# Expert panels in a fused transformer kernel: two sums per panel outside the gate stretch, a shorter routing, new clock estimates

## The chip, the cores and the metric

The kernel runs on one core of a Trainium2 chip. The metric is device time in microseconds (us) from launch to end; three runs of the kernel before took 2847.09, 2847.22 and 2847.55 us, and their median, 2847.22 us, is the time before. The profile is of one further execution.

## The reference, cut to what matters

The program is two blocks of two layers over 256 tokens of width 1024, all in float32. The change touches the last part of each layer of the second block, a product-key expert layer with 16384 experts:

```
def peer(xn, wq, k1, k2, u_tab, v_tab):
    q = (xt @ wq).reshape(t, 8, 256)                    # 8 heads, two halves of 128
    s1, s2 = scores of each half against 128 keys       # einsum with k1, k2
    v1, i1 = lax.top_k(s1, 16); v2, i2 = lax.top_k(s2, 16)
    cand = (v1[..., :, None] + v2[..., None, :]).reshape(t, 8, 256)
    sv, ci = lax.top_k(cand, 16)
    e1 = take_along_axis(i1, ci // 16); e2 = take_along_axis(i2, ci % 16)
    gates = softmax(sv)                                 # expert e1*128+e2, 8*16 per token
    hid = gelu(xi . u_tab[experts]); out = (gates * hid) @ v_tab[experts]
```

The kernel computes this densely: all 16384 hidden values of each token (the u stage), multiplied by a matrix of gates that is zero outside the chosen experts, and then times v_tab (the v stage).

## The kernel before, in words

**Panels.** All weights come in panels of 128x1024 floats, 512 KB, loaded by the SP queue (L63). To hold float32 precision at TensorE's fast rate each panel is split: ScalarE rounds it to fp32r (`whi`), VectorE subtracts (`wlo`). The activations are split the same way, `xh` and `xl`, and lie beside each other in one tile `xhl`. A product is the sum hi*xh + lo*xh + hi*xl. There are three buffers each of `whi` and `wlo`, so VectorE's `wlo` of a panel is put into its queue two panels ahead.

**Two ways to multiply a panel.** `feat` does 24 matmuls of 256 columns into half a PSUM bank, eight for each of the three products; two panels share one bank. `feat_sum` does 8 matmuls of 512 columns (`whi` against xh and xl side by side) and 8 of 256 (`wlo` against xh) into one whole bank, and the two halves are then added by a ScalarE copy and a VectorE add. The feed-forward layers use `feat_sum`; the u stage before uses `feat`.

**The u stage of a layer.** 128 panels, two experts' rows `e`, `e+1` at a time. Beside it, on a queue of chores, run: the search of the 16 best keys per head and half (`firsts`, `top16`: max, max_index, match_replace on VectorE), the routing of the two token halves (`route(0)`, `route(1)`), and then `builds`: 64 steps of 4 tokens. A step has TensorE make a 128x128 gate matrix per token (`gates`: one-hot `ohb` times one-hot `oha` into a bank), VectorE and ScalarE make the one-hots of the next step (`onehots`), and `place` put the gates of the step before into `G` (112 of the expert rows) and `H` (16). Rows whose hidden values exist already (`state["u"]`) are multiplied by the gates on VectorE, the others are copied on ScalarE; `late` does the other side when a pair of panels ends after gates exist: ScalarE's Gelu, and a VectorE multiply for the tokens (`state["t"]`) that have gates. The gates rotate over four PSUM banks, acc00, acc01, acc10, acc11; `feat` uses two banks named `w`.

**What sets the order.** Each engine runs its instructions in the order in which they were written. A `Chains` queue holds the chores as generators; at fixed points (`chains.run()`, three per panel) it issues every step whose due time has passed on a model clock (`Clock`, with `cost` as its price list): the model's end of the step before, plus 0.2 us, less the lead that the step yielded. Every compute instruction is recorded by one helper, so all show as L226.

Of the kernel before, what the change touches and what calls it, by code (L numbers as in the profile page):

```python
# [9 lines left out]
F32 = mybir.dt.float32  # L10
# [22 lines left out]
N_LANES = 4  # L33
EARLY = (0, 1)
LEAD_BUILD = 0.8
LEAD_TOP = 1.0
N_ABS = 2
MIX_ORDER = "FCRAB"
RANK_CONV = 1
RANK_PART = 1  # L40
RANK_RNN = 0
# [85 lines left out]
class Clock:  # L127
# [33 lines left out]
    def cost(self, e, op, out, ins, kw):  # L161
        n = max(math.prod(x.shape[1:]) for x in [out, *ins])
        if e == "p":
            rate = (2 if op == "transpose" else 4) if ins[-1].dtype == F32 else max(1, 256 / out.shape[-1])
            if op == "matmul" and out.shape[0] == 64:
                rate *= 0.6
            return math.prod(out.shape[1:]) * rate / 2.4e3 + 0.003
        if e == "v":
            small = sum(x.shape[1:] == (1,) for x in ins if x.shape != out.shape)
            if op == "tensor_scalar" and ins[0].space == SB:  # L170
                return 0.07 + n / 1.92e3 + 0.06 * small
            return 0.07 + n / 0.96e3 + 0.06 * small
# [116 lines left out]
def net(tc, A, out, stop=None):  # L289
# [3 lines left out]
    with ctx:  # L293
# [8 lines left out]
        def bank():  # L302
            return psum.tile([128, 512], F32, name="w", bufs=2)
# [76 lines left out]

        banks = [0]

        def feat_sum(dst, other):


            banks[0] += 1
            ps = bank() if banks[0] & 2 else other()
            hi, lo = W.get()
            for k in range(8):
                mm(ps, hi[:, k * 128:(k + 1) * 128], xhl[:, :, k], start=k == 0, stop=False)  # L390
                if k == 3:
                    chains.run()
            W.ahead("hi")
            chains.run()
            for k in range(8):
                mm(ps[:, :T], lo[:, k * 128:(k + 1) * 128], xh[:, k], start=False, stop=k == 7)
            W.ahead("lo")
            chains.run()
            nc.scalar.activation(dst, ps[:, T:], AF.Copy)
            nc.vector.tensor_tensor(dst, dst, ps[:, :T], op=OP.add)  # L400

        def nat(ps, xh, xl):

# [879 lines left out]
        def peer(l, acc, soon):  # L1283
            with tc.tile_pool(name=f"peer{l}", bufs=1) as p:
# [77 lines left out]
                def route(c):  # L1362
                    r = R[c]
                    v, i, fi, cf, ef, sv, ci, cs, cand = (r[n] for n in ("v", "i", "fi", "cf", "ef", "sv", "ci", "cs", "cand"))
                    nc.vector.tensor_copy(fi, i)
                    for b in (slice(0, 4), slice(4, 8)):
                        nc.vector.tensor_tensor(cand[:, b], v[:, 0, b][:, :, :, None].to_broadcast([128, 4, 16, 16]),
                                                v[:, 1, b][:, :, None, :].to_broadcast([128, 4, 16, 16]), op=OP.add)
                        yield
                    for h in range(8):  # L1370
                        yield from top16(sv[:, h], ci[:, h], cand[:, h].rearrange("p a b -> p (a b)"))
                        yield LEAD_TOP
                    nc.vector.tensor_scalar(cs, ci, 4, None, op0=OP.logical_shift_right)
                    nc.vector.tensor_copy(cf[:, 0], cs)
                    nc.vector.tensor_scalar(cs, ci, 15, None, op0=OP.bitwise_and)
                    nc.vector.tensor_copy(cf[:, 1], cs)
                    yield
                    for s in range(2):
                        for b in (slice(0, 4), slice(4, 8)):
                            nc.vector.tensor_tensor(cand[:, b], cf[:, s, b][:, :, :, None].to_broadcast([128, 4, 16, 16]),  # L1380
                                                    iota[:, None, None, 0:16].to_broadcast([128, 4, 16, 16]),
                                                    op=OP.is_equal)
                            yield
                            nc.vector.tensor_tensor(cand[:, b], cand[:, b],
                                                    fi[:, s, b][:, :, None, :].to_broadcast([128, 4, 16, 16]), op=OP.mult)
                            yield
                            nc.vector.tensor_reduce(ef[:, s, b], cand[:, b], axis=AX.X, op=OP.add)
                            yield
# [20 lines left out]
                state = {"u": 0, "t": 0}  # L1409

                def onehots(t0):
                    a = p.tile([128, 4, 128], F32, name="oha", bufs=2)
# [11 lines left out]

                def gates(t0, a, b):

                    i = t0 // 4 % 4
                    ps = psum.tile([128, 512], F32, name=f"acc{i // 2}{i % 2}", bufs=1)
                    for j in range(4):
                        mm(ps[:, j * 128:(j + 1) * 128], a[:, j], b[:, j], start=True, stop=True)  # L1430
                    return ps
# [23 lines left out]
                        yield LEAD_BUILD  # L1455
                    place(*last)

                def late(e, ps):

                    nt, g = state["t"], rows(e, 2)  # L1460
                    pv = ps.rearrange("p (a t) -> p a t", a=2)
                    if nt < T:
                        nc.scalar.activation(g[:, :, nt:], pv[:, :, nt:], AF.Gelu_apprx_tanh)
                    if nt:
                        nc.scalar.activation(pv[:, :, :nt], pv[:, :, :nt], AF.Gelu_apprx_tanh)
                        nc.vector.tensor_tensor(g[:, :, :nt], g[:, :, :nt], pv[:, :, :nt], op=OP.mult)
                    state["u"] = e + 2

                for work in (route(0), route(1), builds()):
                    chains.add(work, 1, 1)  # L1470
                for e in range(0, 128, 2):
                    ps = bank()
                    for j in range(2):
                        if e == 80 and j == 0:
                            while state["t"] == 0:
                                chains.idle()
                        feat(ps[:, j * T:(j + 1) * T], xh, xl)
                    late(e, ps)
                chains.drain()
                acc = acc_banks()  # L1480

                def cut(e):
# [44 lines left out]
        def aux(i):  # L1527
            return psum.tile([128, 512], F32, name=f"acc0{i}", bufs=1)
# [170 lines left out]
```

## Time and profile before

| | |
|---|---|
| median of three runs | 2847.22 us |
| the profiled execution | 2847.0 us, of which 2845.2 us span |
| TensorE matmul, busy | 2794.8 us (98%) |
| TensorE weight load, busy | 2553.3 us (90%) |
| VectorE (DVE), busy | 2045.7 us (72%) |
| ScalarE (ACT), busy | 1494.0 us (53%) |
| GpSimd (POOL), busy | 100.7 us (4%) |
| mean granted TensorE clock | 0.992 |

The u stages run from 1104.3 to 1531.1 us (first layer) and from about 2063 to 2489 us. Busy shares are averages over the whole program; a stretch has to be read on its own. Matmuls overlap, so a row's busy time is longer than the distance to the next row's start: the starts tell the pace. The same holds for VectorE.

### The profile page before, as it was taken

How to read it: one execution, taken by the hardware profiler on the slowest of the kernel's cores; microseconds unless marked ns; L12 is line 12 of the kernel's file. 1: busy time of each engine (PE TensorE's matmuls, PEld its weight loads, DVE VectorE, ACT ScalarE, POOL GpSimd, SP SyncE). 2: the span in 40 equal slices, each digit the busy share in tenths (PEclk: the TensorE clock that was granted, in tenths of full speed). 3: DMA queues.
4: the chain of work that ended last, by engine and by line, in shares of the span. 5: the costliest groups of instructions: out<-in, count | busy, mean ns of one | idle time of the engine just before them, and what ended most of it. 6: DMA issues, size and time to landing. Idle time of an engine off the chain costs nothing.

```text
span 2845.2 us, 47840 instructions
## 1 busy us (share of the span) xinstructions
PE 2794.8 (98%) x18786; PEld 2553.3 (90%) x18786; DVE 2045.7 (72%) x3710; ACT 1494.0 (53%) x2423; POOL 100.7 (4%) x104
## 2 busy tenths in 40 slices
PE   9999999999999999999999999999999999999999
PEld 9988889998887889999998888887999999988887
DVE  5556665666766889988995555569898899755555
ACT  4444545544454654447764444456444677544444
POOL 1001010000101100000000000010000000000000
PEclk9999999999999999999999999999999999999999
DMA  6445556544554344554345555543455433455554
GB/s 242 163 164 179 187 176 199 172 148 138 187 192 156 127 144 161 193 181 138 127 138 181 194 195 194 202 159 122 162 180 190 165 127 134 159 190 193 193 194 161
DMA packets 135969, 484.18 MB, mean 170 GB/s; under 512 B 17152, under 2 KB 18176, under 8 KB 135744
## 3 DMA queue, kind: packets, MB, share of 16 engines
q1 hardware_dynamic: 132064, 468.07, 48.2%
q0 software_dynamic: 3680, 13.05, 1.4%
q8 instruction: 148, 2.42, 0.3%
q14 instruction: 77, 0.63, 0.1%
HBM read 479.92 MB, written 1.15 MB: 169 GB/s over the span
## 4 chain that ended last, share of the span: by engine, by line
PE 51%; issue 13%; DVE 2%; ACT 1%; POOL 0%; DVEq 0%; POOLq 0%; ACTq 0%
PE w L226 30%; PE acc L226 19%; DVE G L226 2%; PE b L226 1%; ACT G L226 0%; ACT whi L226 0%; DVE wlo L226 0%; DVE xN L226 0%; ACT ohb L226 0%; POOL r L226 0%; POOL wlo L226 0%; ACT xhl L226 0%; POOL G L226 0%; ACT w L226 0%; DVE nm L226 0%
## 5 line engine op out<-in xcount | busy, mean ns | idle before, releaser
L226 DVE TENSOR_TENSOR wlo<-raw,whi 128x1024 fp32r<-128x1024 f32 (+1 forms) x874 | 1062.6, 1219 | 551.8 <-ACT whi L226 546.1
L226 ACT ACTIVATE whi<-raw 128x1024 fp32r<-128x1024 f32 (+1 forms) x881 | 924.4, 1053 | 673.5 <-PE acc L226 386.4
L226 PE MATMUL w<-xhl,whi 128*128 128x256 f32 (+1 forms) x6176 | 869.5, 292 | 4.4 <-ACT whi L226 4.2
L226 PEld LDWEIGHTS w<-xhl,whi 128*128 128x128 f32 x6176 | 795.4, 193 | 20.8 <-ACT whi L226 5.0
L226 PE MATMUL acc<-whi,xhl 128*128 128x512 f32 x2048 | 550.2, 390 | 2.4 <-ACT xhl L226 2.4
L226 PE MATMUL w<-xhl,wlo 128*128 128x256 f32 x3248 | 462.4, 286 | 9.4 <-DVE wlo L226 9.3
L226 PEld LDWEIGHTS acc<-whi,xhl 128*128 128x128 f32 x2048 | 384.5, 188 | 82.3 <-ACT xhl L226 2.8
L226 PEld LDWEIGHTS w<-xhl,wlo 128*128 128x128 f32 x3248 | 422.5, 193 | 15.4 <-DVE wlo L226 11.2
L226 PE MATMUL acc<-wlo,xhl 128*128 128x512 f32 x1024 | 317.7, 389 | 0.0
L226 PEld LDWEIGHTS acc<-wlo,xhl 128*128 128x128 f32 x1024 | 192.3, 188 | 39.8
L226 ACT ACTIVATE G<-w 128x512 f32<-128x512 f32 (+16 forms) x157 | 81.6, 520 | 203.1 <-PE w L226 202.6
L226 DVE TENSOR_SCALAR oha<-iota,e1T,gT 128x128 f32<-128x128 f32 x512 | 152.8, 341 | 0.0
L226 PE MATMUL acc<-ohb,oha 128*128 128x128 f32 x1024 | 136.7, 276 | 0.3
L226 PEld LDWEIGHTS acc<-ohb,oha 128*128 128x128 f32 x1024 | 125.9, 192 | 2.0 <-ACT ohb L226 1.4
L226 PE MATMUL w<-whi,xhl 128*128 128x256 f32 x640 | 121.2, 287 | 0.0
L226 PEld LDWEIGHTS w<-whi,xhl 128*128 128x128 f32 x640 | 101.9, 193 | 2.3 <-issue 2.1
L226 PE MATMUL w<-wlo,xhl 128*128 128x256 f32 x320 | 91.3, 285 | 0.3
L226 POOL TENSOR_TENSOR r<-v,minus_half 128x1 f32<-128x1 f32 x26 | 21.8, 840 | 1959.5 <-DVE v L226 1959.5
L226 ACT ACTIVATE ohb<-iota,me2T 128x128 f32<-128x128 f32 x256 | 87.5, 392 | 0.7 <-PE acc L226 0.7
L226 PE MATMUL b<-xhl,whi 128*128 128x512 f32 x320 | 80.2, 393 | 0.0
L226 DVE TENSOR_TENSOR xhl<-G,xhl 128x512 fp32r<-128x512 f32 x112 | 76.5, 684 | 0.0
L226 DVE TENSOR_TENSOR G<-G,acc 128x272 f32<-128x272 f32 (+22 forms) x128 | 66.5, 520 | 8.5 <-ACT H L226 8.2
(303 smaller groups left out, 2962.1 us busy)
## 6 DMA issues: line engine op xcount, KB each, us to landing
raw<-u SPq DMA_DIRECT2D x256, 512.0 KB, 3.2
raw<-v SPq DMA_DIRECT2D x256, 512.0 KB, 3.3
raw<-ffn SPq DMA_DIRECT2D x132, 512.0 KB, 4.0
raw<-mix SPq DMA_DIRECT2D x90, 512.0 KB, 3.3
raw<-att SPq DMA_DIRECT2D x80, 512.0 KB, 3.3
raw<-ret SPq DMA_DIRECT2D x63, 512.0 KB, 3.3
bias<-scr POOLq DMA_DIRECT2D x12, 512.0 KB, 7.1
G<-norm_g SPq DMA_DIRECT2D x4, 512.0 KB, 5.6
```

The costliest lines, as they stand in the source:

```text
L226: return f(*args, **kw)
```

## The change

1. `feat_sum` is divided; its matmuls become `feat_both`.
2. In the u stage a panel goes through `feat_both` into one of four banks (the two `w`, acc10, acc11) while no gates are being built, that is before the first `place` and after the last; ScalarE copies and VectorE adds the halves into `u`, a slice of the tile `xN` (`value`), and Gelu reads `u`. Between the first and the last `place` it is `feat`, two panels per bank, as before.
3. The gates keep the two banks acc00 and acc01 (`aux`).
4. `xN`, which holds the residual, is saved to DRAM ahead of this and loaded back after the u stage, on GpSimd's queue.
5. `route` no longer adds all 256 pairs of each head but 52 that can be among the best 16, in lists of 64; the index passes are smaller or rewritten.
6. `Clock.cost` prices max, max_index and match_replace at 0.2 us more than the size term in place of 0.07; `LEAD_TOP` goes from 1.0 to 2.0, and `route`'s steps yield a lead of 2.0.

```diff
+        if e == "v" and op in ("max", "max_index", "match_replace"):
+            return 0.2 + n / 0.96e3
...
-        def feat_sum(dst, other):
+        def feat_both(ps):
             hi, lo = W.get()
             for k in range(8):
                 mm(ps, hi[:, k * 128:(k + 1) * 128], xhl[:, :, k], start=k == 0, stop=False)
...
+        def feat_sum(dst, other):
+            banks[0] += 1
+            ps = bank() if banks[0] & 2 else other()
+            feat_both(ps)
             nc.scalar.activation(dst, ps[:, T:], AF.Copy)
             nc.vector.tensor_tensor(dst, dst, ps[:, :T], op=OP.add)
+            chains.run()
...
+                kept = dram.tile([128, 2, D], F32, name=f"kept{l}")
+                nc.gpsimd.dma_start(kept, xN)
...
+                    for o, a0, na, nb in RANKS:
+                        sh = [128, 8, na, nb]
+                        nc.vector.tensor_tensor(few[:, :, o:o + na * nb].rearrange("p h (a b) -> p h a b", a=na),
+                                                v[:, 0, :, a0:a0 + na, None].to_broadcast(sh),
+                                                v[:, 1, :, None, 0:nb].to_broadcast(sh), op=OP.add)
+                    yield LEAD_ROUTE
...
-                    i = t0 // 4 % 4
-                    ps = psum.tile([128, 512], F32, name=f"acc{i // 2}{i % 2}", bufs=1)
+                    ps = aux(t0 // 4 % 2)
...
+                def value(e, j, u, ps):
+                    nc.scalar.activation(u[:, j], ps[:, T:], AF.Copy)
+                    yield
+                    nc.vector.tensor_tensor(u[:, j], u[:, j], ps[:, :T], op=OP.add)
+                    state["b"] += 1
+                    if j:
+                        yield
+                        late(e, u)
...
                 for e in range(0, 128, 2):
-                    ps = bank()
+                    if 0 < state["t"] < T:
+                        while state["b"] < state["s"]:
+                            chains.idle()
+                        ps = bank()
+                        for j in range(2):
+                            feat(ps[:, j * T:(j + 1) * T], xh, xl)
+                        late(e, ps.rearrange("p (a t) -> p a t", a=2))
+                        continue
+                    u = hid[:, state["s"] // 2 % 4]
                     for j in range(2):
...
+                        ps = bank() if n & 2 else psum.tile([128, 512], F32, name=f"acc1{n % 2}", bufs=1)
+                        feat_both(ps)
+                        chains.add(value(e, j, u, ps), "value", 0)
                 chains.drain()
+                nc.gpsimd.dma_start(xN, kept)
```

What this does to the order is the same in both layers; all before the first u stage is unchanged on every engine. In TensorE's queue before, the stretch with gates settles to four gate groups (`ohb,oha`, four tokens each) in three panels (a panel is `whi` x8, `wlo` x8, `whi` x8; x16 spans the end of one and the start of the next):

```order
L226 MATMUL w<-xhl,whi 128x256 x16
L226 MATMUL w<-xhl,wlo 128x256 x8
L226 MATMUL acc_13341<-ohb,oha 128x128 x4
L226 MATMUL w<-xhl,whi 128x256 x16
L226 MATMUL acc_13378<-ohb,oha 128x128 x4
L226 MATMUL w<-xhl,wlo 128x256 x8
L226 MATMUL acc_13409<-ohb,oha 128x128 x4
L226 MATMUL w<-xhl,whi 128x256 x16
L226 MATMUL w<-xhl,wlo 128x256 x8
```

After, the same place has the last panels in two sums (512 columns), and then two gate groups in every panel:

```order
L230 MATMUL acc_13063<-ohb,oha 128x128 x4
L230 MATMUL acc_13058<-xhl,whi 128x512 x4
L230 MATMUL acc_13058<-xhl,wlo 128x256 x8
L230 MATMUL acc_13105<-ohb,oha 128x128 x4
L230 MATMUL w<-xhl,whi 128x256 x8
L230 MATMUL w<-xhl,wlo 128x256 x8
L230 MATMUL acc_13149<-ohb,oha 128x128 x4
L230 MATMUL w<-xhl,whi 128x256 x16
L230 MATMUL acc_13189<-ohb,oha 128x128 x4
L230 MATMUL w<-xhl,wlo 128x256 x8
L230 MATMUL acc_13220<-ohb,oha 128x128 x4
```

The groups have moved together: the 64 of a layer lie in 47 panels before and in 32 after, of which the last 30 have two each. Before, 67 panels come ahead of the first group and 14 after the last; now 77 and 19, with 96 of the 128 panels in two sums and 32 by `feat`.

In VectorE's queue before, in the same stretch, a `wlo` stands after every one or two build steps (a step is four `oha`, two `ohb` and the multiply of `place`):

```order
L226 TENSOR_TENSOR wlo<-raw,whi 128x1024
L226 TENSOR_SCALAR oha<-iota,e1T,gT 128x128 x3
L226 TENSOR_SCALAR ohb<-miota,me2T 128x128
L226 TENSOR_SCALAR oha<-iota,e1T,gT 128x128
L226 TENSOR_SCALAR ohb<-miota,me2T 128x128
L226 TENSOR_TENSOR G<-G,acc_13257 128x68x4
L226 TENSOR_TENSOR G<-G,w 128x2x16
L226 TENSOR_TENSOR wlo<-raw,whi 128x1024
```

After, two full steps stand between one `wlo` and the next throughout, and the multiply of `late` (`G<-G,w`) in every second panel:

```order
L230 TENSOR_TENSOR wlo<-raw,whi 128x1024
L230 TENSOR_SCALAR oha<-iota,e1T,gT 128x128 x3
L230 TENSOR_SCALAR ohb<-miota,me2T 128x128
L230 TENSOR_SCALAR oha<-iota,e1T,gT 128x128
L230 TENSOR_SCALAR ohb<-miota,me2T 128x128
L230 TENSOR_TENSOR G<-G,acc_14169 128x92x4
L230 TENSOR_TENSOR G<-G,w 128x2x132
L230 TENSOR_SCALAR oha<-iota,e1T,gT 128x128 x3
L230 TENSOR_SCALAR ohb<-miota,me2T 128x128
L230 TENSOR_SCALAR oha<-iota,e1T,gT 128x128
L230 TENSOR_SCALAR ohb<-miota,me2T 128x128
L230 TENSOR_TENSOR G<-G,acc_14200 128x94x4
```

## Rows read from the trace of the kernel before

**Rows 1.** Windows: length, busy us of PE, PEld, DVE, ACT, POOL; clock, DMA
```profile
1104.30:1298.00 193.70, 193.70 (x1617) 193.70 (x1617) 171.04 (x355) 95.26 (x111) 0.00 (x0) 1.00 0.53 183
1299.00:1491.00 192.00, 191.85 (x1630) 191.14 (x1630) 181.38 (x515) 142.56 (x404) 0.00 (x0) 1.00 0.38 131
```
**Rows 2.** TensorE's timeline, u stage without gates: start, busy us, engine, operation
```profile
1245.78 2.08 PE L226 MATMUL w<-xhl,whi 128*128 128x256 f32 x16
1248.66 2.08 PE L226 MATMUL w<-xhl,whi 128*128 128x256 f32 x16
```
**Rows 3.** TensorE's timeline, gate stretch: a panel with two groups, then with one
```profile
1304.08 2.16 PE L226 MATMUL w<-xhl,whi 128*128 128x256 f32 x16
...
1308.73 2.16 PE L226 MATMUL w<-xhl,whi 128*128 128x256 f32 x16
...
1312.50 2.16 PE L226 MATMUL w<-xhl,whi 128*128 128x256 f32 x16
```
**Rows 4.** The u stage's first and the v stage's first matmul, with ScalarE between
```profile
1104.26 2.16 PE L226 MATMUL w<-xhl,whi 128*128 128x256 f32 x16
...
1529.97 0.58 ACT L226 ACTIVATE w<-w 128x512 f32<-128x512 f32 x1 [1.82 <-PE w L226]
1530.47 1.14 ACT L226 ACTIVATE xhl<-G 128x512 fp32r<-128x512 f32 x2
1531.14 0.73 PE L226 MATMUL acc<-whi,xhl 128*128 128x512 f32 x2 [1.21 <-ACT xhl L226]
```
**Rows 5.** TensorE's timeline, feed-forward layer: two panels of `feat_sum`
```profile
305.93 2.00 PE L226 MATMUL b<-xhl,whi 128*128 128x512 f32 x8
...
311.52 1.78 PE L226 MATMUL w<-xhl,whi 128*128 128x512 f32 x7
```
**Rows 6.** VectorE's timeline, gate stretch: `wlo`, a step, the next step, a wait
```profile
1303.18 1.22 DVE L226 TENSOR_TENSOR wlo<-raw,whi 128x1024 fp32r<-128x1024 f32 x1
1304.32 0.85 DVE L226 TENSOR_SCALAR oha<-iota,e1T,gT 128x128 f32<-128x128 f32 x3
...
1305.73 0.43 DVE L226 TENSOR_TENSOR G<-G,acc 128x272 f32<-128x272 f32 x1
1306.08 0.85 DVE L226 TENSOR_SCALAR oha<-iota,e1T,gT 128x128 f32<-128x128 f32 x3
...
1307.77 0.44 DVE L226 TENSOR_TENSOR G<-G,acc 128x272 f32<-128x272 f32 x1 [0.18 <-ACT H L226]
```
**Rows 7.** VectorE's groups, 1104 to 1535 us: busy us, mean ns, idle before, releaser
```profile
L226 DVE TENSOR_TENSOR H<-H,w 128x512 f32<-128x512 f32 x7 | 4.8, 689 | 7.5 <-ACT w L226 7.5
L226 DVE TENSOR_TENSOR G<-G,acc 128x368 f32<-128x368 f32 x3 | 1.6, 537 | 0.4 <-ACT H L226 0.4
L226 DVE TENSOR_TENSOR G<-G,w 128x264 f32<-128x264 f32 x1 | 0.4, 417 | 0.0
```
**Rows 8.** TensorE's timeline at the first two gate groups
```profile
1297.94 1.12 PE L226 MATMUL w<-xhl,whi 128*128 128x256 f32 x8
1299.07 1.56 PE L226 MATMUL acc<-ohb,oha 128*128 128x128 f32 x8
1300.38 1.20 PE L226 MATMUL w<-xhl,whi 128*128 128x256 f32 x8
```
**Rows 9.** Feed-forward layer: ScalarE's copy and VectorE's add after a `feat_sum` panel
```profile
308.93 0.39 ACT L226 ACTIVATE g<-b 128x256 f32<-128x256 f32 x1 [1.46 <-PE b L226]
...
309.34 0.42 DVE L226 TENSOR_TENSOR g<-g,b 128x256 f32<-128x256 f32 x1 [0.62 <-ACT g L226]
```
**Rows 10.** VectorE's timeline, key searches in lists of 128: first half, second half, next
```profile
1107.41 0.29 DVE L226 MAX8 G<-G 128x8 f32<-128x128 f32 x1
...
1108.52 0.29 DVE L226 MAX8 G<-G 128x8 f32<-128x128 f32 x1
...
1109.13 0.28 DVE L226 MAX8 G<-G 128x8 f32<-128x128 f32 x1
```
**Rows 11.** DMA issues: KB each, median us from issue to landing
```profile
xN<-x POOLq DMA_DIRECT2D x1, 1024.0 KB, 12.7
```

More of the change, by code (lines that the diff above doesn't have):

```diff
@@ L35 @@
 LEAD_BUILD = 0.8
-LEAD_TOP = 1.0
+LEAD_TOP = 2.0
+LEAD_ROUTE = 2.0
 N_ABS = 2
 MIX_ORDER = "FCRAB"
+RANKS = ((0, 0, 1, 16), (16, 1, 1, 8), (24, 2, 2, 8), (40, 4, 4, 4), (56, 8, 8, 1))
 RANK_CONV = 1
@@ L381, in net @@
         banks = [0]
-        def feat_sum(dst, other):
-            banks[0] += 1
-            ps = bank() if banks[0] & 2 else other()
+        def feat_both(ps):
             hi, lo = W.get()
@@ L1365, in route @@
                     nc.vector.tensor_copy(fi, i)
[L1366 to L1369, printed above, removed]
+                    flat = cand.rearrange("p h a b -> p (h a b)")
+                    few = flat[:, :512].rearrange("p (h n) -> p h n", h=8)
@@ L1370, in route @@
+                    for o, a0, na, nb in RANKS:
[4 more added lines that the diff above has]
+                    yield LEAD_ROUTE
                     for h in range(8):
-                        yield from top16(sv[:, h], ci[:, h], cand[:, h].rearrange("p a b -> p (a b)"))
+                        yield from top16(sv[:, h], ci[:, h], few[:, h])
@@ L1372, in route @@
                         yield LEAD_TOP
[L1373 to L1377, printed above, removed]
-                    for s in range(2):
[L1379 to L1388, printed above, removed]
+                    t0, t1, t2 = (flat[:, j * 128:(j + 1) * 128].rearrange("p (h k) -> p h k", h=8) for j in range(3))
@@ new lines, in route @@
+                    ra, rb = cf[:, 0], cf[:, 1]
+                    nc.vector.tensor_copy(t0, ci)
+                    for t, n in ((t1, 3), (t2, 2)):
+                        nc.vector.tensor_scalar(cs, ci, n, None, op0=OP.logical_shift_right)
+                        nc.vector.tensor_copy(t, cs)
+                    yield LEAD_ROUTE
+                    nc.vector.tensor_scalar(t1, t1, -1.0, 0.0, op0=OP.add, op1=OP.max)
+                    nc.vector.scalar_tensor_tensor(t1, t2, -6.0, t1, op0=OP.add, op1=OP.max)
@@ new lines, in route @@
+                    nc.vector.scalar_tensor_tensor(ra, t0, -48.0, t1, op0=OP.add, op1=OP.max)
+                    yield LEAD_ROUTE
+                    nc.vector.tensor_scalar(t1, ra, 8.0, 8.0, op0=OP.mult, op1=OP.add)
+                    nc.vector.scalar_tensor_tensor(t1, ra, 16.0, t1, op0=OP.mult, op1=OP.min)
+                    nc.vector.tensor_scalar(t2, ra, 4.0, 24.0, op0=OP.mult, op1=OP.add)
+                    nc.vector.scalar_tensor_tensor(t2, ra, 48.0, t2, op0=OP.add, op1=OP.min)
+                    nc.vector.tensor_tensor(t1, t1, t2, op=OP.min)
@@ new lines, in route @@
+                    nc.vector.tensor_tensor(rb, t0, t1, op=OP.subtract)
+                    yield LEAD_ROUTE
+                    for s in range(2):
+                        for k0, nr in ((0, 8), (8, 16)):
+                            q = flat[:, :64 * nr].rearrange("p (h k a) -> p h k a", h=8, k=8)
+                            sh, ks = [128, 8, 8, nr], slice(k0, k0 + 8)
+                            nc.vector.tensor_tensor(q, cf[:, s, :, ks, None].to_broadcast(sh),
+                                                    iota[:, None, None, 0:nr].to_broadcast(sh), op=OP.is_equal)
+                            yield LEAD_ROUTE
+                            nc.vector.tensor_tensor(q, q, fi[:, s, :, None, 0:nr].to_broadcast(sh), op=OP.mult)
+                            yield LEAD_ROUTE
+                            nc.vector.tensor_reduce(ef[:, s, :, ks], q, axis=AX.X, op=OP.add)
+                            yield LEAD_ROUTE
@@ L1407, in route @@
                     yield
-                state = {"u": 0, "t": 0}
+                state = {"u": 0, "t": 0, "b": 0, "s": 0}
                 def onehots(t0):
@@ L1456, in builds, with late @@
                     place(*last)
-                def late(e, ps):
+                def late(e, pv):
                     nt, g = state["t"], rows(e, 2)
-                    pv = ps.rearrange("p (a t) -> p a t", a=2)
                     if nt < T:
@@ L1470, in peer @@
                     chains.add(work, 1, 1)
-                for e in range(0, 128, 2):
-                    ps = bank()
-                    for j in range(2):
[L1474 to L1478, printed above, removed]
+                def value(e, j, u, ps):
[6 more added lines that the diff above has]
+                        late(e, u)
+                hid = xN.rearrange("p c (i a t) -> p (c i) a t", i=2, a=2)
+                for e in range(0, 128, 2):
+                    if e == 80:
+                        while state["t"] == 0:
+                            chains.idle()
+                    if 0 < state["t"] < T:
+                        while state["b"] < state["s"]:
+                            chains.idle()
+                        ps = bank()
[4 more added lines that the diff above has]
+                    u = hid[:, state["s"] // 2 % 4]
+                    for j in range(2):
+                        n = state["s"]
+                        state["s"] += 1
+                        while n - state["b"] > 3:
+                            chains.idle()
+                        ps = bank() if n & 2 else psum.tile([128, 512], F32, name=f"acc1{n % 2}", bufs=1)
+                        feat_both(ps)
+                        chains.add(value(e, j, u, ps), "value", 0)
                 chains.drain()
+                nc.gpsimd.dma_start(xN, kept)
                 acc = acc_banks()
```

## The prediction, made before the changed kernel had run

> **What bounds the kernel now.** Read the windows first. In the stretch of a u stage that has no gates yet, TensorE and its weight loads are busy all of 193.70 us and VectorE 171.04; in the stretch with gates TensorE 191.85 of 192.00 and VectorE 181.38, that is 94% [rows 1]. The clock is granted in full in both. Then TensorE's timeline, by starts: without gates a panel of `feat` takes 1248.66 - 1245.78 = 2.88 us [rows 2]. With gates, the panel with two groups takes 1308.73 - 1304.08 = 4.65 and the one with one 1312.50 - 1308.73 = 3.77 [rows 3], so a group costs 0.887. Of the whole stage: 128 x 2.88 + 64 x 0.887 = 425.4 us, and 1.2 of idle time ahead of the v stage make 426.6; from its first matmul to the v stage's first it takes 1531.14 - 1104.26 = 426.9 [rows 4]. So TensorE never waits for long inside the stage, though VectorE is close behind it. The reader is to see that: one engine full, a second at nine tenths, and a change that takes work from the first and gives some to the second.
>
> **The change on TensorE.** A panel in two sums takes (311.52 - 305.93) / 2 = 2.795 us where the feed-forward layer does it now [rows 5]; 16 weight loads in place of 24, but the same columns, so it gains only 0.085 us on 2.88. In the order, 96 panels of a layer go that way and 32 stay with `feat`: 96 x 2.795 + 32 x 2.88 + 56.8 (groups) = 417.3 us. TensorE alone would gain 8.1 us per layer.
>
> **The change on VectorE where gates are built.** Here the order matters more than the matmuls: the gate groups stand two to a panel for 30 panels, where four stood in three. TensorE needs 4.65 us for such a panel. VectorE, again by starts: `wlo` 1304.32 - 1303.18 = 1.14; the six one-hot instructions of a step 1305.73 - 1304.32 = 1.41; the multiply of `place` at 272 elements 1306.08 - 1305.73 = 0.35 [rows 6]. A next instruction thus starts 0.08 us ahead of the end that its row shows. The multiply grows with the rows done, in the order from 74 to 108 of them with four tokens each, mean 92: 368 elements take 537 ns [rows 7], 0.45 by starts. `late`'s multiply has from 0 to 512 elements, mean 256; 264 take 417 ns [rows 7], 0.34 by starts, in every second panel. The sum for a panel is 1.14 + 2 x 1.41 + 2 x 0.45 + 0.34 / 2 = 5.03 us, against TensorE's 4.65: 0.38 too much, 11.3 us over 30 panels. In the order before, three panels held 3 x 1.14 + 4 x (1.41 + 0.45) + 0.5 = 11.4 us on VectorE and 12.2 on TensorE, which is why nothing waits today.
>
> Can TensorE run ahead and take this excess from stock? `wlo` alone would allow it to be some 4.6 us late, since it stands two panels ahead. But a gate group needs its bank: with two banks in place of four, group k writes where group k-2 was, and the multiply that empties that bank is the last VectorE instruction of the step just ahead. So each group waits until VectorE has ended that step, and behind the group in TensorE's queue stand all later panels. I count the full 11.3. No row shows a group in want of a bank, as four were always enough; the ends are 11.3 - 4.6 = 6.7 and 11.3, and I take the upper, because the dependence is in the order itself.
>
> The Trainium skill says in "Perfetto Trace Analysis", section "Optimizing Tensor Performance", that independent matmul groups should rotate through different PSUM banks so that the evacuation of one overlaps the next. The change goes from four to two here. By that rule the 11.3 is paid in full; without it, 6.7. No run here shows either yet.
>
> **VectorE's own waits.** In the gate stretch it waits now and then for ScalarE, 0.18 us before a `place` [rows 6]; behind it, seven multiplies of `late` waited 7.5 us in all [rows 7]. ScalarE does about 1.0 (`whi`), two steps of 1.3 and half of two Gelus, 4 us in a panel of 5, but its Gelus must wait for the panel's end and `whi` stands behind them. From nothing to 0.6 us in every two panels, 0 to 9 us; I take 4, the nearest being the 0.4 us that three multiplies waited for [rows 7] and the 0.18. The first groups have their one-hots in the same step as the matmuls; before, TensorE lost 1300.38 - 1299.07 - 0.89 = 0.4 and, ahead of it, 0.2 [rows 8]. After, the `wlo` ahead of them is just issued too: up to 1.6, I take 0.5 more.
>
> **The end of the stage.** Now Gelu of the last pair follows its panel, and then the first `xhl`, 0.50 us later [rows 4]. After, a copy of 0.39 and an add of 0.42 come between panel and Gelu [rows 9], with two hand-overs of 0.04 (309.34 - 308.93 - 0.39 is 0.02): 0.9 us more, and nothing covers it.
>
> **Costed at nothing.** The stretch without gates: VectorE gets an add of 0.34 per panel and loses list work. A search takes 1108.52 - 1107.41 = 1.11 us for its first half and 1109.13 - 1108.52 = 0.61 for its second in lists of 128 [rows 10]; the 64-long lists are not in the trace and cost no more than these, and not less than the fixed part. With 77 `wlo` (87.8), 74 adds (25.2), 35 first and 36 second halves (60.8), 24 index passes (21.6: 12 like a `wlo`, 12 half) and some 53 small ones at 0.25 (13), VectorE has 208 us of work in TensorE's 77 x 2.795 = 215. So TensorE covers it, at 97%: if it did not, see the third rival. The smaller routing work does not bring the gates forward: 77 panels come ahead of them, 67 before, since the steps are priced higher and issued later, and 2.88 x 67 = 193 us became 215. The copy and Gelu on ScalarE: it was busy 95 of 194 us there [rows 1] and gets 77 x 0.3 more. The two transfers of `xN`: 1 MB, 12.7 us to land when last done [rows 11], with DMA at 0.38 to 0.53 [rows 1]; the saved copy has 50 us, the other the whole v stage; if the loads of panels are pushed back for its time, the ring of four panels (4 x 2.7 us) covers it. Uncovered, it would be up to 5 us per layer. All before the first u stage, and the v stages, keep their order.
>
> **The sum.** Per layer: 417.3 + 1.2 + 0.9 (end) + 11.3 + 0.5 + 4 = 435.2 us, against 426.9: 8.3 slower. Two layers: 16.6. The profiled execution took 2847.0 us, which is the median of the runs within 0.3, so 2847.0 + 16.6 = 2863.6. Its own bounds: without waits and with a clean start 417.3 + 2.1 + 11.3 = 430.7, 3.8 per layer, 2855; with 9 of waits, 1.6 at the start and 2 of small stalls in the first stretch 443.3, 16.4 per layer, 2880.
>
> **Rivals.**
> First, VectorE keeps up, because an instruction overlaps its neighbour more when the queue is never empty: then only TensorE's gain and the end count, 417.3 + 2.1 = 419.4, 7.5 per layer, 2832 us: faster. For it: TensorE waited for nothing in 192 us with VectorE at 94%. Against: the starts of rows 6 are those of a queue that was not empty. It decides if a panel with two groups costs VectorE under 4.65.
> Second, the banks don't bind, and the two panels of `wlo` in stock are used up first: 417.3 + 2.1 + 6.7 + 0.5 = 426.6, no change, 2846 us. Against: the bank is a wait in the order.
> Third, VectorE is short in the first stretch as well: an add waits for its ScalarE copy, 0.3 us per panel on an engine at 97%, so 0.16 over TensorE's pace; 75 panels make 12 us per layer more, 2888 us. For it: the thin cover. Against: VectorE's queue lags behind TensorE there, so the copy is done when the add's turn comes.
>
> **Chances.** The forecast 0.74, first rival 0.09, second 0.09, third 0.08. About 0.2%, 5.7 us, is what the measurement can tell from no change. Faster 0.10, same 0.10 (the second, and a little of the forecast's lower end), slower 0.80. The range from 2846 to 2880 takes in the forecast's own (2855 to 2880) and the second rival; the first and the third stay out.
>
> **What would show it.** In the new profile: panels of 2.795 us ahead of the gates, VectorE near 100% and TensorE below 95% where they are built, 5.0 to 5.3 us per panel with two groups, and waits of TensorE's groups for VectorE's `G`. Wrong if such panels take 4.65, or if TensorE waits for `wlo` ahead of the gates.

## The result: 33 us slower, twice the forecast

The changed kernel took 2880.48 us (median of four runs, 2879.64 to 2880.88), the kernel before 2847.15 in the same comparison (four runs): a ratio of 1.0112, 95% interval 1.0099 to 1.0124. Forecast were 2863.6 us and 16.6 us of loss; measured are 33.3. The direction was right, the forecast loss was half of the measured one, and the time lies 0.5 us above the 2880 us at which the stated range ended.

The profiled execution of the changed kernel has a span of 2878.4 us; the line is the page's busy time of each engine, its share and its instructions.

```profile
PE 2800.9 (97%) x17250; PEld 2475.9 (86%) x17250; DVE 2073.4 (72%) x3944; ACT 1548.6 (54%) x2611; POOL 100.0 (3%) x108
```

Over the whole span this hardly differs from before. The windows of the first u stage show where to look (columns as in [rows 1]): the stretch without gates, the stretch with two groups to a panel, and the end of the stage.

```profile
1097.74:1312.00 214.26, 214.26 (x1233) 188.59 (x1232) 191.44 (x499) 129.35 (x199) 0.00 (x0) 1.00 0.62 188
1324.20:1486.00 161.80, 149.51 (x1180) 140.51 (x1179) 152.27 (x459) 112.64 (x351) 0.00 (x0) 1.00 0.33 97
1489.00:1543.00 54.00, 53.92 (x319) 47.68 (x318) 37.70 (x48) 30.57 (x48) 0.00 (x0) 1.00 0.59 179
```

TensorE is full in the first and the third window. In the second **no engine is full**: TensorE has 92%, VectorE 94%, ScalarE 70%, at a clock granted in full. That is the sign of a loop of waits, and not of an engine that is too slow. From the last group of key scores to the v stage the first layer took 427.7 us before and 445.5 after, the second layer the same to 0.02 us: 17.8 us more in each. The part from the first gate group to the last took 191.4 us before, for 46 2/3 panels and 63 groups (TensorE alone: 46 2/3 x 2.88 + 63 x 0.887 = 190.3), and 173.8 after for 32 panels (148.0). So 25.7 us of each layer are waits there, where before there were 1.1.

The terms that came out as forecast first. The pace ahead of the gates (TensorE's timeline, as [rows 5]):

```profile
1201.99 2.00 PE L230 MATMUL acc<-xhl,whi 128*128 128x512 f32 x8
...
1204.78 1.55 PE L230 MATMUL w<-xhl,whi 128*128 128x512 f32 x6
```

2.79 us per panel, as taken from the feed-forward layer. The first matmul of the v stage (it answers the last row of [rows 4]), and the two transfers of `xN` (KB each, median us to landing):

```profile
1545.04 0.73 PE L230 MATMUL acc<-whi,xhl 128*128 128x512 f32 x2 [2.11 <-ACT xhl L230]
...
kept<-xN POOLq DMA_DIRECT2D x2, 1024.0 KB, 4.3
xN<-kept POOLq DMA_DIRECT2D x2, 1024.0 KB, 6.0
```

TensorE stood idle 2.11 us there in place of 1.21: the 0.9 that copy and add cost at the end. The transfers land in 4.3 and 6.0 us and nothing waits for them.

**The loop, in the rows.** First TensorE's timeline in the gate stretch, where [rows 3] showed 4.65 us from one panel to the next:

```profile
1339.49 1.13 PE L230 MATMUL acc<-ohb,oha 128*128 128x128 f32 x8
1340.37 2.16 PE L230 MATMUL w<-xhl,whi 128*128 128x256 f32 x16
1342.44 1.13 PE L230 MATMUL acc<-ohb,oha 128*128 128x128 f32 x8
1343.33 1.19 PE L230 MATMUL w<-xhl,wlo 128*128 128x256 f32 x8
1345.34 1.13 PE L230 MATMUL acc<-ohb,oha 128*128 128x128 f32 x8 [0.81 <-DVE G L230]
1346.22 0.48 PE L230 MATMUL w<-xhl,whi 128*128 128x256 f32 x2
...
1351.38 1.80 PE L230 MATMUL w<-xhl,whi 128*128 128x256 f32 x13
```

then ScalarE's in the same time:

```profile
1341.61 0.54 ACT L230 ACTIVATE G<-w 128x440 f32<-128x440 f32 x1 [1.49 <-PE w L230]
1342.18 0.21 ACT L230 ACTIVATE w<-w 128x72 f32<-128x72 f32 x1
1342.31 1.05 ACT L230 ACTIVATE whi<-raw 128x1024 fp32r<-128x1024 f32 x1
1343.26 0.68 ACT L230 ACTIVATE ohb<-iota,me2T 128x128 f32<-128x128 f32 x2
1343.97 0.42 ACT L230 ACTIVATE ohb<-ohb 128x256 f32<-128x256 f32 x1
1344.30 0.25 ACT L230 ACTIVATE G<-acc 128x120 f32<-128x120 f32 x1
1344.45 0.21 ACT L230 ACTIVATE H<-acc 128x64 f32<-128x64 f32 x1
```

and VectorE's `place` at its end:

```profile
1344.69 0.50 DVE L230 TENSOR_TENSOR G<-G,acc 128x328 f32<-128x328 f32 x1 [0.61 <-ACT H L230]
```

Read it as one chain. The group at 1339.49 holds TensorE for 0.88 us; behind it comes the last third of its panel, which ends at about 1341.3. ScalarE has waited 1.49 us for that end: it does the Gelu of the pair (0.70), `whi` (0.95), the one-hots (1.04) and the copies of `place` (0.39), in the order in which they are queued. Only then comes VectorE's multiply of `place`, which had waited 0.61 us; it frees the bank, and at 1345.34 TensorE starts the group that wanted this bank, after 0.81 us of waiting. From group to group 1345.34 - 1339.49 = 5.85 us, and the group that is late makes the next panel's end late. Where no pair ended, the Gelu is missing: from 1346.22 to 1351.38 it is 5.16, which is 5.85 less 0.70 within 0.01. The mean of the two is 5.50. The waits of the window (total us, times, longest) name three engines that wait for each other in a ring:

```profile
ACT G L230 <- PE w L230: 23.5, 15, 1.7
ACT whi L230 <- PE w L230: 23.3, 15, 1.7
PEld acc L230 <- issue: 19.4, 41, 1.0
PE acc L230 <- DVE G L230: 11.1, 15, 0.8
DVE G L230 <- ACT H L230: 7.8, 24, 0.7
```

Only 11.1 us of TensorE's waits carry the name of the multiply. The 19.4 us of `issue` ahead of the groups' weight loads have no releaser in the profile: the group at 1339.49 is not marked as waiting, and yet it starts 0.15 us behind the end of a multiply of `place` (1338.85 + 0.49), as the group at 1345.34 does (1344.69 + 0.50).

### The profile page after: what moved, and what is told of

It reads as the page before. It is cut to its first block, busy times and chain, and to the rows that moved or that the text cites. A ratio compares the mean times of both kernels' runs of the same rounds, so it can differ in the third digit from the quotient of the medians.

```text
span 2878.4 us, 45424 instructions
## 1 busy us (share of the span) xinstructions
PE 2800.9 (97%) x17250; PEld 2475.9 (86%) x17250; DVE 2073.4 (72%) x3944; ACT 1548.6 (54%) x2611; POOL 100.0 (3%) x108
## 5 line engine op out<-in xcount | busy, mean ns | idle before, releaser
L230 PE MATMUL w<-xhl,whi 128*128 128x256 f32 (+1 forms) x3872 | 655.3, 317 | 3.5 <-ACT whi L230 3.3
L230 PEld LDWEIGHTS w<-xhl,whi 128*128 128x128 f32 x3872 | 548.8, 192 | 44.4 <-ACT whi L230 4.1
L230 PE MATMUL w<-xhl,wlo 128*128 128x256 f32 x2480 | 355.2, 286 | 8.9 <-DVE wlo L230 8.9
L230 PEld LDWEIGHTS w<-xhl,wlo 128*128 128x128 f32 x2480 | 328.5, 192 | 22.9 <-DVE wlo L230 11.2
L230 PE MATMUL acc<-xhl,whi 128*128 128x512 f32 (+1 forms) x832 | 202.1, 384 | 0.0
L230 PE MATMUL acc<-ohb,oha 128*128 128x128 f32 x1024 | 145.0, 284 | 26.0 <-DVE G L230 22.8
L230 PEld LDWEIGHTS acc<-xhl,whi 128*128 128x128 f32 x832 | 145.9, 189 | 24.4
L230 PEld LDWEIGHTS acc<-xhl,wlo 128*128 128x128 f32 x800 | 108.7, 190 | 7.4
L230 PE MATMUL acc<-xhl,wlo 128*128 128x256 f32 x800 | 111.9, 283 | 0.0
L230 DVE TENSOR_TENSOR G<-G,acc 128x320 f32<-128x320 f32 (+17 forms) x128 | 68.6, 536 | 16.8 <-ACT H L230 15.6
```

The lines of the kernel that those rows point to most:

```text
L230: return f(*args, **kw)
```

## The experiments

The edits are shown shortened, against the changed kernel or, where it is said, against the kernel before.

Theory A was this loop, closed by the two gate banks. Theory B was that VectorE's work with its own waits sets the 5.50, whatever the banks are. The order of the instructions could be held fixed while banks changed, because these runs give the model clock a table in which a bank's name can be replaced by another; so order and banks could be varied apart.

**Four gate banks, the changed kernel's order.**

```
-  ps = aux(t0 // 4 % 2)
+  i = next of acc00, acc01, acc10, acc11   # acc1x only once no sum is pending in them
+  ps = psum.tile([128, 512], F32, name=f"acc{i // 2}{i % 2}", bufs=1)
+  clock.alias[ps.tensor.name] = f"acc0{t0 // 4 % 2}"   # the model clock still counts two
```

> The changed kernel with its gate groups on four banks again (acc00, acc01, acc10, acc11) from the third group on; every engine's order is word for word that of the changed kernel, only the bank names differ. Theory A, the loop through two banks: a panel with two groups takes 5.50 us because each second group waits for the place that empties its bank, which waits for ScalarE, which waits for the end of the panel that this very group delays. Four banks open the loop, and what is left is VectorE's own work, 5.03 to 5.2 us per panel: 9 to 14 us less per layer, 2852 to 2862 us. Theory B, VectorE's work with its waits for ScalarE sets the 5.50 whatever the banks are: 2880 +-3 us and 5.4 to 5.6 us per panel.

2855.25 us (eight runs; ratio to before 1.0028, 1.0018 to 1.0039): 25 us less than the changed kernel by a change of bank names alone. The stretch from the first gate group to the last went from 173.8 to 159.2 us. Its window, a gate group near its end, and its longest waits (from 1324 to 1470 us):

```profile
1315.21:1474.42 159.21, 159.20 (x1265) 152.32 (x1266) 159.21 (x497) 122.47 (x380) 0.00 (x0) 1.00 0.35 107
...
1463.06 1.56 PE L231 MATMUL acc<-ohb,oha 128*128 128x128 f32 x8
...
ACT G L231 <- PE w L231: 17.1, 14, 1.4
ACT whi L231 <- PE w L231: 13.5, 15, 1.3
PEld acc L231 <- DVE ohb L231: 2.2, 14, 0.2
```

The waits of TensorE for `G` are gone, VectorE is busy all of 159.21 us, and TensorE waits a little for its one-hots. TensorE's own 159.20 us of busy time hide pauses: by its pace it needs 148.0, and a gate group, whose row lasts 1.05 to 1.06 us early in the stretch, lasts up to 1.56 where its matmuls wait for VectorE's `ohb` (the last line names 2.2 us of these waits). Now, and only now, VectorE is the bound: 159.2 / 32 = 4.98 us per panel, where the forecast's sum was 5.03. Theory A holds for 14.6 of the 25.7 us; the other 11.2 stand with a VectorE that is never idle, and the run with the shorter `place` below tests them. The Trainium skill says in "Perfetto Trace Analysis", section "Optimizing Tensor Performance", that independent groups should rotate through PSUM banks; the trace agrees, at 14.6 us per layer between two banks and four.

**Two banks and four at a slower rate.** With four banks in the model clock the planner itself spreads the groups over 50 panels in place of 32. That order was run with both numbers of banks.

```
 # run 1: four banks as above, without the alias
 # run 2: ps = aux(t0 // 4 % 2); clock.alias[ps.tensor.name] = one of four names
```

> The changed kernel with two gate banks as it has, but the gate groups spread over 50 panels in place of 32, about four groups in three panels as in the kernel before. Theory A: with only every third panel holding two groups, the loop has slack, and TensorE alone counts: 78 x 2.795 + 50 x 2.88 + 56.8 + 4.2 (the first panel's score matmuls and small idle times, as before) + 0.9 at the end = 423.9 per layer against 429.6, so 5.7 less per layer, 2834 to 2840 us. Theory B gives the same here, since three panels hold 11.4 us of VectorE's work and 12.2 of TensorE's. Theory C, two banks bind at any rate: 2850 us or more, with waits of TensorE for G of over 10 us per layer.

> The same order as the run with 50 panels and two gate banks, word for word, with four gate banks. Theory A and B: within 3 us of that run, at 2834 to 2838 us, since the loop has slack there with two banks already. Theory C: 10 us or more faster than it.

Two banks took 2845.50 us (eleven runs; ratio 0.9996, 0.9986 to 1.0005), four 2832.07 (five runs; 0.9947, 0.9933 to 0.9960). The windows from first group to last, two banks and then four:

```profile
1315.83:1522.98 207.15, 204.19 (x1697) 200.77 (x1697) 192.30 (x540) 144.63 (x400) 0.54 (x1) 1.00 0.42 133
```

```profile
1316.61:1517.59 200.98, 200.84 (x1696) 199.82 (x1697) 191.32 (x540) 144.32 (x400) 0.54 (x1) 1.00 0.43 137
```

TensorE alone needs 50 x 2.88 + 63 x 0.887 = 199.9. With four banks 1.1 us are waits, as in the kernel before; with two 7.3. The first run missed its 2834 to 2840 us, so I was wrong that the loop has slack at this rate: where groups stand close, as they still do every few panels, the run with two banks falls back by 0.2 to 0.9 us each time. Four banks are 13.4 us faster than two (6.2 in the stretch of each layer), which is what theory C said of that pair; its own figure for two banks, 2850 us and more, was too high. The run with four banks is the version that beats both kernels: 14 us under the one before, 48 under the changed one.

**Part 3 alone.** The kernel before with nothing but the two gate banks.

```
-  i = t0 // 4 % 4
-  ps = psum.tile([128, 512], F32, name=f"acc{i // 2}{i % 2}", bufs=1)
+  ps = aux(t0 // 4 % 2)
```

> The kernel before with part 3 of the change alone: the gates on acc00 and acc01; every panel through feat, old routing, old prices. The model clock counts the wait for a bank into TensorE's time, so steps fall due sooner, and the gate groups come to stand over 31 panels in place of 47: two to a panel, as in the changed kernel. If the loop through two banks is the whole loss, it appears here without any of the other parts: the stretch from the first gate group to the last as in the changed kernel, some 170 us, where TensorE alone needs 31.3 x 2.88 + 55.9 = 146; 24 us more per layer, 2893 to 2897 us (the changed kernel has 8 us less per layer from the two sums, and it is at 2880). Rival: part of the loss needs the two sums as well (banks and buffers that the sums hold when the gates begin): under 2885 us.

2897.46 us (five runs; 1.0182, 1.0169 to 1.0196), 0.5 above the upper end of the expectation: one line costs 52 us, more than the whole change. The window from first group to last, and the waits from 1300 to 1465 us:

```profile
1297.54:1469.96 172.42, 158.54 (x1257) 149.85 (x1257) 159.91 (x491) 123.07 (x374) 0.00 (x0) 1.00 0.29 98
```

```profile
ACT whi L226 <- PE w L226: 22.6, 15, 1.6
ACT G L226 <- PE w L226: 22.4, 15, 1.6
...
PE acc L226 <- DVE G L226: 11.8, 17, 0.8
DVE G L226 <- ACT H L226: 10.4, 29, 0.7
```

The same ring, with 172.4 us where TensorE needs 31 1/3 x 2.88 + 55.9 = 146.1: 26.3 of waits. And the order moved too: 31 panels hold the groups, 47 before. The planner adds a wait for a bank to its clock of TensorE; with two banks that clock runs ahead, more steps are due at each point, and the groups are put closer together, which is what two banks bear least. The runs above show the same from the other side: there only the names that the model clock sees went from two to four, and 32 panels became 50.

**Parts 5 and 6 alone.** The kernel before with the shorter routing, its leads and the prices of searches.

```
+LEAD_TOP = 2.0; LEAD_ROUTE = 2.0; RANKS = ...
+        if e == "v" and op in ("max", "max_index", "match_replace"):
+            return 0.2 + n / 0.96e3
+                def route(c): as changed
```

> The kernel before with parts 5 and 6 of the change alone: the shorter routing, its leads and the search prices; every panel goes through feat, and the gates have four banks and stand after the same panels as before. The account so far (all of the loss stands where gates are built, none of it comes from routing): 2847 +-3 us. Rival: the routing work that goes from VectorE lets something else run sooner, or the issue of many small steps costs TensorE waits: over 5 us away from the kernel before on either side.

2845.34 us (eleven runs; 0.9992, 0.9983 to 1.0001): no difference that can be told. The gates stand after the same panels, and the stage took 427.2 us where it took 427.7. (By `RANKS` in the kernel the shorter routing adds 64 pairs of each head, and not the 52 named with the change.)

**Gelu out of the loop, two banks.**

```
     for j in range(2):
-        feat(ps[:, j * T:(j + 1) * T], xh, xl)
-    late(e, ps...)
+        feat(..., then=lambda: held and late(*held.pop()))   # after the second third
+    held.append((e, ps...))
```

> The changed kernel, two gate banks, two groups per panel, but the Gelu of a pair of panels with gates is written after the second third of the next panel, so that it stands behind whi and the one-hots in ScalarE's queue and not ahead of them. Theory A, the loop through two banks: ScalarE's Gelu is part of the loop only where it stands between the panel's end and whi; the panel with Gelu goes from 5.85 to the 5.16 of the other, 15 x 0.69 = 10 us less per layer, 2856 to 2864 us. Rival: the loop needs ScalarE's whole work of two panels whatever its order, and the Gelu only moves on: 2876 to 2882 us.

2864.28 us (five runs; 1.0063, 1.0050 to 1.0077), 16 less than the changed kernel. TensorE's starts of panels, without and with a pair's end:

```profile
1349.25 2.16 PE L230 MATMUL w<-xhl,whi 128*128 128x256 f32 x16
...
1354.41 2.16 PE L230 MATMUL w<-xhl,whi 128*128 128x256 f32 x16
...
1359.57 2.16 PE L230 MATMUL w<-xhl,whi 128*128 128x256 f32 x16
```

Both take 5.16 us now. The numbers of instructions are the same. With the Gelu the multiply of `late` moved too and covers four tokens more; it was not in the chain above, where VectorE still had 0.61 us to wait behind it. The stretch fell by 8.0 us, the stage by 8.9, where 10 were expected: towards the end of the stretch the panels with a pair's end grow again, to 5.49 us. VectorE is busy 162.32 of 165.80 us from first group to last; whether that is why was not tried.

**Less work on VectorE, by GpSimd.** Half of each `wlo` goes to GpSimd while gates are built, with two banks and with four.

```
-  vector.tensor_tensor(lo, r, hi, op=subtract)
+  gpsimd.tensor_tensor(lo[:, :512], r[:, :512], hi[:, :512], op=subtract)
+  vector.tensor_tensor(lo[:, 512:], r[:, 512:], hi[:, 512:], op=subtract)
```

> The changed kernel, two gate banks, but while gates are built half of each wlo (512 of 1024 columns) is subtracted on GpSimd, which is idle there; VectorE has about 0.55 us less per panel, 16 us per layer. Theory A: VectorE is not what ends a panel while the loop does; 5.50 us per panel stays but for the little that VectorE's place starts late behind its own work: 2870 to 2882 us. Theory B, VectorE's own work sets part of the 5.50: about 0.35 us off each panel, 2858 to 2862 us. If GpSimd is slow beside VectorE, wlo comes late and it is slower than 2882.

> The same with the gate groups on four banks, order word for word that of the changed kernel. With the loop open, the stretch from the first gate group to the last took 159.2 us per layer, 11.2 more than TensorE needs for its 32 panels and 63 groups (148.0). If these 11.2 are VectorE's work, as forecast, taking 0.55 us per panel from it leaves TensorE as the bound: 148 to 151 us, 2834 to 2840 us. Rival: the 11.2 are waits for ScalarE (whi, one-hots, copies), then they stay: 2852 to 2857 us.

2912.73 us with two banks (five runs; 1.0234, 1.0220 to 1.0248) and 2881.14 with four (four runs; 1.0121, 1.0105 to 1.0136). The first lies above both of its ranges, in the case that it named for a slow GpSimd; the second missed both of its ranges. The edit did not take time from VectorE. VectorE's and GpSimd's timelines, two banks:

```profile
1347.09 1.31 DVE L237 TENSOR_SCALAR oha<-iota,e1T,gT 128x128 f32<-128x128 f32 x1
1348.32 0.27 DVE L237 TENSOR_SCALAR ohb<-miota,me2T 128x128 f32<-128x128 f32 x1
...
1352.57 1.38 DVE L237 TENSOR_SCALAR ohb<-miota,me2T 128x128 f32<-128x128 f32 x1
```

```profile
1346.99 1.32 POOL L87 TENSOR_TENSOR wlo<-raw,whi 128x512 fp32r<-128x512 f32 x1 [4.58 <-PE acc L237]
1352.45 1.42 POOL L87 TENSOR_TENSOR wlo<-raw,whi 128x512 fp32r<-128x512 f32 x1 [4.14 <-ACT whi L237]
```

A one-hot of about 0.3 us that comes 0.1 us behind GpSimd's start lasts until GpSimd's end: 1.31 us, and 1.38 the next time. The 0.5 us saved on `wlo` (1.22 to 0.68) come back as 1.0 us of standing still; the stretch grew by 14.2 us with two banks and by 13.4 with four, 0.4 for each of 32 panels. These two runs tell nothing of A or B.

**Less work on VectorE, by leaving it out.** Four banks, the changed kernel's order; the multiply of `place` covers 8 expert rows only, so this kernel leaves the gates of the other rows out.

```
-  nc.vector.tensor_tensor(g[:, :m - a], g[:, :m - a], pv[:, a:m], op=OP.mult)
+  nc.vector.tensor_tensor(g[:, :8], g[:, :8], pv[:, a:a + 8], op=OP.mult)   # priced in full
```

> The changed kernel with four gate banks in its own order, and the place multiply cut to its first 8 expert rows, 32 elements in place of 296 to 432; it leaves the gates of the other rows out. VectorE has about 0.3 us less per multiply, 0.6 us per panel. With the loop open, VectorE was busy in all of the stretch; its 4.98 us per panel become about 4.35, under TensorE's 4.65: the stretch goes from 159.2 to 148 to 150 us, 2832 to 2838 us. Rival: what is left of the 11.2 us is not VectorE's work: 2850 us or more.

2839.88 us (eleven runs; 0.9979, 0.9970 to 0.9988). The window from first group to last, and two of the waits in it:

```profile
1316.03:1469.05 153.02, 152.14 (x1265) 148.68 (x1266) 142.74 (x498) 122.32 (x380) 0.00 (x0) 1.00 0.37 111
```

```profile
PEld acc L231 <- ACT ohb L231: 3.7, 14, 0.3
ACT ohb L231 <- PE acc L231: 2.2, 1, 2.2
```

Of the 11.2 us 6.2 are gone, not all. VectorE is at 93% now, and panels take 4.65 us or, in every second panel, about 4.98: the next wait, 14 times 0.3 us, is for ScalarE's one-hots. That VectorE's work costs time is shown for 6.2 of the 11.2; in the run with four banks it was busy all the time, so the waits that make up the other 5.0 lay behind it unseen, and no run in this order takes them away.

**Every panel in two sums.** The gates rotate over acc00, acc01, b0 and b1, so that the sums keep their four banks in the gate stretch.

```
-  if 0 < state["t"] < T: ... feat(...) ...
-  ps = aux(t0 // 4 % 2)
+  ps = psum.tile(..., name=("acc00", "acc01", "b0", "b1")[t0 // 4 % 4], bufs=1)
```

> Every panel in two sums, in the stretch with gates too; the gates rotate over acc00, acc01, b0 and b1 and stand over 51 panels. TensorE: 2.795 + 1.255 x 0.887 = 3.91 us per panel. VectorE by the same sum as in the forecast: 1.14 + 0.34 + 1.255 x 1.86 + 0.17 = 3.98. If both are right, it gains 51 x 0.085 = 4.3 and loses 51 x 0.07 = 3.6 us per layer against the run with 50 panels and four banks: 2829 to 2833 us. Rival: the adds bring a new wait of VectorE for ScalarE's copies inside the stretch: 5 us or more per layer, over 2840 us.

2859.47 us (five runs; 1.0049, 1.0035 to 1.0063): over the rival's 2840, but not by its mechanism, since VectorE waited for ScalarE's copies for 3.1 us in 176 (1324 to 1500 us). While there are panels TensorE is full: the planner puts one group to most panels. But then 13 groups are left when the last panel is done. TensorE's timeline among the panels and at the last groups:

```profile
1351.25 2.09 PE L230 MATMUL w<-xhl,whi 128*128 128x512 f32 x8
...
1354.94 2.09 PE L230 MATMUL w<-xhl,whi 128*128 128x512 f32 x8
...
1526.55 1.56 PE L230 MATMUL b<-ohb,oha 128*128 128x128 f32 x8 [0.52 <-DVE oha L230]
1528.63 1.96 PE L230 MATMUL b<-ohb,oha 128*128 128x128 f32 x8 [0.52 <-DVE oha L230]
```

A panel with its group takes 3.69 us, as 2.795 + 0.887 would have it. Windows of the stretch, of its end, and of a part of that end:

```profile
1400.00:1450.00 50.00, 50.00 (x327) 45.27 (x325) 48.39 (x130) 38.52 (x110) 0.00 (x0) 1.00 0.46 140
```

```profile
1515.00:1532.00 17.00, 12.57 (x60) 9.78 (x58) 16.63 (x63) 7.13 (x19) 0.00 (x0) 0.80 0.00 1
1522.00:1528.60 6.60, 4.87 (x26) 3.36 (x26) 6.60 (x26) 3.33 (x9) 0.00 (x0) 1.00 0.00 0
```

These groups come 2.08 us apart at VectorE's pace, with no panel beside them, 25 us for the twelve steps from the first to the last, where TensorE's pace of 0.887 makes 10.6. The 14.4 us between them, twice, are about the 28 us by which the run lies above the middle of its expectation. The expectation had taken the planner's 51 panels for an even spread, which the order doesn't show.

## Why the prediction was right in its sign and half its size

**TensorE's own gain**, 8.1 us per layer: right within 0.4. From the parts of the stage, 215.37 (ahead of the gates) + 148.04 (32 panels, 63 groups) + 56.32 (from the last group on) is 419.73, where the same sum of before is 195.62 + 190.28 + 40.65 = 426.55. That is 6.8 less, with the 0.9 of the stage's end paid in it, so 7.7.

**The rows for the stage's start** were read one panel late: the last key scores stand inside the first u panel, which begins 2.7 us ahead of the matmul in [rows 4]. The stage had some 4 us outside its panels and groups and not 1.2; as both kernels have it, the difference does not feel it.

**VectorE's excess**, 11.3 us per layer: right in size. With the loop open the stretch has 11.2 more than TensorE needs, and VectorE is full in it. The sum by starts, 5.03 us per panel, was 4.98. In the changed kernel itself, though, this excess does not set the pace: VectorE is at 94% there, and the ring makes 5.50 us. Of the signs that the forecast named, TensorE under 95% (92%) and its waits for `G` came; VectorE near 100% and 5.0 to 5.3 us per panel did not. So the slower time alone would not have spoken for the 11.3; the run with four banks does.

**The third rival**, VectorE short ahead of the gates: refuted, 191.44 of 214.26 us busy; my 208 was too high, and TensorE never waits there. The first and second rival fell with the 173.8 us.

**VectorE's own waits for ScalarE**, "from nothing to 0.6 us in every two panels, 0 to 9 us; I take 4": this is the term that was mis-sized. It measured 14.6 us per layer, outside its bounds, by the difference between two banks and four in one order. With it the sum is 0.5 + 11.3 + 14.6 = 26.4, less the 1.1 of waits that before had, so 25.3, against 24.6 measured, and per layer -7.7 + 0.9 + 24.6 = 17.8, which is what each of the two stages lost. That the time came out within 0.5 us of the range's end is luck: its 2880 was made of 9 us of these waits, 1.6 at the first groups and 2 of stalls ahead of the gates, where TensorE was in fact full in all of 214.26 us.

The fault was not a wrong row. The dependence was named: a group waits for the multiply that empties its bank, and all later panels stand behind the group. I counted what VectorE's lateness costs through that wait, and bounded ScalarE's part by short waits in a trace where four banks kept the ring open. I did not follow the ring to its start: the multiply waits for ScalarE's copies, these stand behind `whi` and Gelu, and these wait for the end of the very panel that the group delays. Added up from the changed kernel's rows, with their hand-overs, group, last third, Gelu, `whi`, one-hots, copies and `place` make 5.85 us for a panel, and 5.16 without the Gelu, where I had 5.03 as the larger of two engines' sums. The same kinds of instruction stand in the trace of before.

The 35.5 us of the two u stages and the 33.2 us by which the two spans differ are 2.3 apart: the changed kernel's profiled execution was some 4 us ahead when the first u stage began, where both kernels have the same order, and from its first v stage to the second layer's key scores it took 1.5 longer, but not behind the second v stage. The granted clock goes the same way: up to the first u stage it was 0.98 before and 0.99 after; in the 15 us from 1545.00 on, behind TensorE's 2.11 us of idle time, it was 0.89, so part of them at 1.2 GHz, and 1.00 (2.4 GHz) in the 15 us from 1531.00 on before. Neither difference was tried apart.

## What to carry to other kernels

When buffers between engines become fewer, do not only compare the engines' sums: write down the chain from one use of a buffer to the next use of the same buffer, across all engines and in queue order, and divide its length by the number of buffers (here 5.85 us over two banks, 2.93 for each group, and a panel has two); the pace can be no faster than the largest of that and of the sums. A stretch where no engine is full, and three of them wait in a ring, is the mark of it in a profile. A planner that counts waits into its clock may answer a shortage of buffers by packing the work closer, so after such a change read the new order before anything else; here one line of bank names cost 52 us, and giving two banks back made the change worth 14.

## What the runs showed of the hardware

GpSimd, idle in the u stages, was no help to VectorE: each of its subtractions of 512 columns took 1.34 us in the mean of 27, against 0.68 for VectorE's half, and held two VectorE one-hots of about 0.3 us for 1.31 and 1.38 us, until GpSimd was done. The Trainium skill says in "SBUF — State Buffer", section "Who interferes with whom", that VectorE shares one of its two pairs of ports with GpSimd, and that against a VectorE instruction in a two-port mode, which `tensor_scalar` can enter, whichever is issued first holds that pair for its whole instruction while the other stands still. The rows agree with that: GpSimd began at 1346.99 and 1352.45, the one-hots 0.10 and 0.12 us later. In which mode the one-hots ran no row shows.

In the last groups of the run with every panel in two sums, TensorE did nothing but gate groups with idle time between them, and the granted clock was 0.80 in that window, so part of it at 1.2 GHz, against 1.00, 2.4 GHz throughout, in the one with panels. The longer rows of the groups are not all the clock's: the group at 1526.55 lasts 1.56 us where 1.00 was granted, since its matmuls wait for one-hots; the one at 1528.63 lasts 1.96, and from 1528.60 to 1532.00 the granted clock was 0.52.
